# TensorE alone in text order in the phases of seven products, and another order of pieces in the convolution (a two-layer trunk on one core)

## The chip, the core and the metric

One core of a Trainium2 chip runs the whole program in one launch. Its engines are TensorE (PE in the profile; PEld is its weight load), VectorE (DVE), ScalarE (ACT), GpSimd (POOL) and SyncE (SP), which issues the transfers. Each engine works off its own list of instructions in order and waits on semaphores for the others. The metric is the device time of one execution in microseconds (us), as the median of several runs.

## What is computed

Two layers work on x of 1024 positions by 1024 channels in float32: the first mixes the positions by attention with a forgetting gate, the second by a convolution module, and after each mixer comes a gated MLP with a short convolution.

```
x = x + fox_attention(rms_norm(x))                 # layer 0, 16 heads of 64
x = x + conv_ffn(rms_norm(x))
x = x + conformer_conv(rms_norm(x))                # layer 1
x = x + conv_ffn(rms_norm(x))

def conformer_conv(h):                             # 1024 channels, 31 taps
    u = h @ w_pw1 + b_pw1
    a, g = split(u)
    u = causal_dwconv(a * sigmoid(g), w_dw) + b_dw
    return silu(rms_norm(u, ln_g)) @ w_pw2 + b_pw2

def conv_ffn(h):                                   # F = 2816, 3 taps
    u = causal_dwconv(h @ w_up, w_dw) + b_dw       # w_up: 1024 x 5632
    gate, val = split(u)
    return (silu(gate) * val) @ w_down             # w_down: 2816 x 1024
```

## The kernel before

**Products in three parts.** A float32 operand is split into a high part in TensorE's fp32r type (a cast on ScalarE, line 266) and a low part, the rest (a subtraction on GpSimd or VectorE, line 267). A product is then three matmuls (lines 272 to 274, `mm3`): high by high, low by high, high by low. Buffers of weights are few: 8 raw tiles of 256 KB (`raw`), 8 high and 8 low parts (`whi`, `wlo`).

**The up-projection in seven products.** `up` makes the product of a tile of 128 features by all 1024 positions with Strassen's scheme in Winograd's form: the 2x2 block product (halves of the 1024 inputs by halves of the positions) takes seven products of 12 matmuls each instead of eight. GpSimd makes the sums of the weights' quarters s1 to s4 (line 471). The sums on the activations' side are made once ahead, by `combine`. The 22 tiles (each: 128 gate features as upper row, 128 value features as lower row) go through this in a fixed order. TensorE's order in the steady state is product 6 of the next tile, 4 and 3 of the present one, then 5 and 7 of the next one; a "full" tile has products 1 and 2 besides. Products 6, 7 and 4 add up in one PSUM bank (`y`), 5 and 3 in another (`z`). Between them VectorE reads the bank's state: u2 after product 6 (line 533), u3 after product 7 (line 542), c22, the lower right block, from z and u3 (line 543). So product 4 can start only when u3 has been read out of `y`. After product 4 y gets its last addend (line 547), after product 3 z does (line 556).

Each of a tile's four blocks then goes through the three taps: ScalarE makes the last tap and the bias (line 483), copies or adds the two edge columns between the halves of positions (lines 486 and 491), VectorE adds the other two taps (line 493, twice). The gate's two blocks go through Silu on ScalarE (line 497), and VectorE multiplies gate by value (line 502); the result is stored in DRAM (`actd`, line 194).

**Early products.** Products 1 and 2 of a tile need no sums. `early` makes them ahead: beside `combine`, and in layer 1 also beside the convolution; ScalarE copies them out of PSUM (line 437), they are stored (`p1d`, `c11d`) and fetched again by the tile (line 476). Such a tile is called "ready" here; it has five products, and its x block comes from SBUF. In layer 0, 13 of 22 tiles are ready, in layer 1 all.

**Ahead.** In layer 0 each full tile also splits `AHEAD` = 4 weight tiles for later (`split_ahead`, lines 309 to 316): load, cast on ScalarE, subtraction on VectorE (line 315), store of the low part. They are the 32 tiles of the convolution's `w_pw1` (which both of its halves use) and the first 4 rows of the second down-projection. Who uses them later loads the low part instead of subtracting (line 85).

**The down-projection** (`down`) runs for each half of the positions and each half of the outputs over 22 rows: activations and weights are both split, VectorE making one low part and GpSimd the other; 12 matmuls a row.

**The convolution** (`conv`) runs for each half of the positions over 8 tiles of 128 channels. `glu` makes the two products (4 pieces, 48 matmuls) and then the gate piece: sigmoid on ScalarE (line 1045), the product u on VectorE (line 1048). `taps_of` does the 31 taps: 10 of them as products on ScalarE (line 1084) and sums on GpSimd (line 1085), 21 on VectorE (lines 1078 and 1080) in seven pieces, then the end piece: y, the sum of both (line 1092), its square on ScalarE (lines 1094 and 1097), added up on GpSimd (line 1098). In the list two pieces of taps stand to one of the next tile's `glu`; every 4 pieces of the first half's list one row of the second down-projection follows (`CONV_DOWN`), every 5 of the second half's list one early product (`CONV_FILL`).

**What sets the order.** The attention and its output projection are ordered by the compiler's scheduler. All that follows is a list of pieces (`pieces` and `trace`): loads stand ahead of splits, splits ahead of the work on TensorE, and the whole stretch stands in one `manual_schedule()`: every engine's list keeps the order of the text.

## Time and profile before

| | us |
|---|---|
| median of 3 runs | 2701.33 |
| range of the runs | 2698.57 to 2701.36 |
| the profiled execution | 2692.02 |
| its span | 2690.3 |
| PE busy in it | 2356.1 (88%) |
| DVE, ACT, POOL busy | 1616.4, 1381.5, 1401.8 |

The stretches, from the first and last instructions of their lines in the trace: attention and its output projection to 667 us; early products and `combine` to 742; tiles of layer 0's up-projection to 1211; first down-projection to 1339; first convolution with the second down-projection to 1641; second product of the convolution to 1663; second convolution to 1858; its norm, second product and `combine` to 2007; tiles of layer 1's up-projection to 2434; down-projections to the end. A busy PE in these lists is not PE at its peak: the end of a matmul is modelled, and at full clock matmuls start closer together than their listed lengths.

### The profile page before, as it was taken

Reading aid. Unit: us, or ns where it says so; the run is one execution under the profiler, and the core shown is the slowest. Engines: PE = TensorE matmul, PEld = TensorE weight load, DVE = VectorE, ACT = ScalarE, POOL = GpSimd, SP = SyncE. Lnnn points to the kernel's source line nnn. Section 1 sums busy time; section 2 is a strip of 40 time slices with the busy share of each in tenths; the row PEclk is TensorE's granted clock in tenths of the full one; section 3 lists DMA queues with packets and bytes.
Section 4 is the critical chain, followed back from the end, with each engine's and each line's share of the span. In section 5 each row is a group of like instructions: output and inputs, shape, how many; then the busy total and the mean of one; then the engine's idle time right before and its main releaser. Section 6 shows DMA issues by size and latency. Waiting matters only on the chain. (4 is left out here: it accounts for less than half of the span.)

```text
span 2690.3 us, 35380 instructions
## 1 busy us (share of the span) xinstructions
PE 2356.1 (88%) x11282; PEld 1993.4 (74%) x11282; DVE 1616.4 (60%) x2855; ACT 1381.5 (51%) x2956; POOL 1401.8 (52%) x1220
## 2 busy tenths in 40 slices
PE   7999999999987778889988978787977777778998
PEld 6899999977865667667866767676866666567887
DVE  5577777763745566665258973786475555555232
ACT  5566666653544445554455554555444444445443
POOL 2455554430165656655557764576255565554543
PEclk9999999999999989999999989898988888889999
DMA  4222222432633334556665446353543333335674
GB/s 118 58 77 82 82 80 69 166 113 85 221 110 99 110 98 146 160 171 228 200 212 163 147 133 196 110 164 113 189 129 102 107 105 98 98 117 193 194 256 157
DMA packets 355083, 366.70 MB, mean 136 GB/s; under 512 B 24872, under 2 KB 246864, under 8 KB 354896
## 3 DMA queue, kind: packets, MB, share of 16 engines
q1 hardware_dynamic: 354896, 364.44, 42.9%
q8 instruction: 89, 1.46, 0.2%
q14 instruction: 98, 0.80, 0.1%
HBM read 281.44 MB, written 74.51 MB: 132 GB/s over the span
## 5 line engine op out<-in xcount | busy, mean ns | idle before, releaser
L267 POOL TENSOR_TENSOR wlo<-raw,whi 128x512 fp32r<-128x512 f32 (+1 forms) x322 | 462.9, 1444 | 318.8 <-ACT whi L266 294.3
L266 ACT CAST whi<-raw 128x512 fp32r<-128x512 f32 (+2 forms) x544 | 326.2, 632 | 284.2 <-PE dn L273 193.8
L272 PE MATMUL y<-bhi,whi 128*128 128x512 f32 x528 | 239.0, 453 | 193.6 <-DVE u L542 179.2
L267 POOL TENSOR_TENSOR wlo<-s,whi 128x512 fp32r<-128x512 f32 x176 | 234.0, 1341 | 304.3 <-ACT whi L266 272.0
L267 DVE TENSOR_TENSOR wlo<-raw,whi 128x512 fp32r<-128x512 f32 (+1 forms) x222 | 187.3, 850 | 278.0 <-ACT whi L266 265.1
L272 PE MATMUL dn<-whi,whi 128*128 128x512 f32 x704 | 280.0, 398 | 16.7 <-ACT whi L266 10.6
L272 PEld LDWEIGHTS y<-bhi,whi 128*128 128x128 f32 x528 | 116.0, 220 | 235.7 <-ACT whi L266 181.8
L273 PE MATMUL dn<-wlo,whi 128*128 128x512 f32 x704 | 279.1, 396 | 12.0 <-POOL wlo L267 7.5
L274 PE MATMUL dn<-whi,wlo 128*128 128x512 f32 x704 | 278.4, 396 | 1.3 <-DVE wlo L267 1.3
L1080 DVE SCALAR_TENSOR_TENSOR cacc<-u,ctaps,cacc 128x512 f32<-128x512 f32 x320 | 241.7, 755 | 10.7
L273 PE MATMUL y<-blo,whi 128*128 128x512 f32 x528 | 232.2, 440 | 0.0
L274 PE MATMUL y<-bhi,wlo 128*128 128x512 f32 x528 | 230.3, 436 | 0.3 <-POOL wlo L267 0.3
L1085 POOL TENSOR_TENSOR pacc<-pacc,prod 128x512 f32<-128x512 f32 x144 | 193.0, 1340 | 51.1 <-ACT prod L1084 43.7
L266 ACT CAST whi<-s 128x512 fp32r<-128x512 f32 x176 | 104.5, 612 | 182.6 <-POOL s L471 182.6
L145 POOL TENSOR_SCALAR ss<-ss 128x4 f32<-128x4 f32 (+1 forms) x96 | 21.2, 221 | 327.2 <-ACT hn L160 178.6
L272 PE MATMUL pj<-whi,hthi 128*128 128x384 f32 (+1 forms) x512 | 180.0, 352 | 6.0 <-ACT sqr L736 3.5
L273 PE MATMUL pj<-wlo,hthi 128*128 128x384 f32 (+1 forms) x512 | 178.0, 348 | 0.5 <-DVE wlo L267 0.5
L274 PE MATMUL pj<-whi,htlo 128*128 128x384 f32 (+1 forms) x512 | 178.2, 348 | 0.0
L272 PEld LDWEIGHTS dn<-whi,whi 128*128 128x128 f32 x704 | 134.7, 191 | 48.4 <-ACT whi L266 12.6
L273 PEld LDWEIGHTS dn<-wlo,whi 128*128 128x128 f32 x704 | 134.9, 192 | 42.6 <-POOL wlo L267 9.7
L471 POOL TENSOR_TENSOR s<-raw,raw 128x512 f32<-128x512 f32 x88 | 116.8, 1327 | 83.6 <-DMA raw<-in_ffn_w_up_dram 60.3
L274 PEld LDWEIGHTS dn<-whi,wlo 128*128 128x128 f32 x704 | 135.0, 192 | 30.2 <-DVE wlo L267 1.8
(217 smaller groups left out, 6322.2 us busy)
## 6 DMA issues: line engine op xcount, KB each, us to landing
raw<-in_ffn_w_up_dram SPq DMA_DIRECT2D x246, 256.0 KB
raw<-actd SPq DMA_DIRECT2D x176, 256.0 KB
raw<-in_ffn_w_down_dram SPq DMA_DIRECT2D x176, 256.0 KB
raw<-in_conv_w_pw_dram SPq DMA_DIRECT2D x96, 256.0 KB
actd<-acc SPq DMA_DIRECT2D x88, 256.0 KB
wlo<-pwlo SPq DMA_DIRECT2D x64, 256.0 KB
raw<-in_fox_w_in_dram SPq DMA_DIRECT2D x64, 192.0 KB
xd<-x SPq DMA_DIRECT2D x24, 512.0 KB
```

Source lines behind the costliest of these rows:

```text
L145: nc.gpsimd.tensor_scalar(ss, ss, 1.0 / n, EPS, op0=ALU.mult, op1=ALU.add)
L266: self.nc.scalar.copy(hi, raw)
L267: (self.nc.vector if vector else self.nc.gpsimd).tensor_tensor(lo, raw, f32(hi), op=ALU.subtract)
L272: nc.tensor.matmul(out, lh, rh, start=start, stop=False, skip_group_check=more)
L273: nc.tensor.matmul(out, lh, rl, start=False, stop=False, skip_group_check=more)
L274: nc.tensor.matmul(out, ll, rh, start=False, stop=stop, skip_group_check=more)
L471: nc.gpsimd.tensor_tensor(st[o], *(st[m].rearrange("p a b -> p (a b)") if m[0] == "a" else st[m] for m in ((y, x) if o == "s4" else (x, y) ...
L1080: nc.vector.scalar_tensor_tensor(acc, win(j), tap(j), acc, op0=ALU.mult, op1=ALU.add)
L1085: nc.gpsimd.tensor_tensor(pacc, pacc, p, op=ALU.add)
```

## The change

1. `manual_schedule` is opened anew by a piece `order(...)`. In the two up-projections (from the end of `combine`) it names TensorE alone; ScalarE, VectorE, GpSimd and SyncE get the order that the compiler's scheduler gives them. After the first one all engines keep text order again; after the second one nothing is switched back, so the last two down-projections belong to it too. `combine` itself stays in text order, with two early products to each of its first six pieces and one to each of the last six (before: two to each).
2. In the convolution pieces of taps and of `glu` alternate one to one, so that the gate piece stands amid the taps; the square of a tile is a piece of its own, after the third piece of the next tile's taps. In the second half the products of two tiles come first.
3. `CONV_FILL` is (6, 1), `AHEAD` is 5, and the numbers of pieces around the second half are others.
4. The bias `b_pw2` is added by VectorE instead of GpSimd.

```diff
-CONV_FILL = (5, 1)
+CONV_FILL = (6, 1)
-AHEAD = 4
+AHEAD = 5
...
+    def order(self, *engines):
+        def run():
+            if self.region is not None:
+                self.region.__exit__(None, None, None)
+            self.region = self.tc.manual_schedule(engines=set(engines) if engines else None)
+            self.region.__enter__()
+        return Piece(run)
...
                 nc.vector.tensor_tensor(y, t["acc"], t["pacc"], op=ALU.add)
-                if ct == 0:
-                    nc.scalar.activation(st["sqa"], y, AF.Square)
-                else:
-                    sq = self.part("sq")
-                    nc.scalar.activation(sq, y, AF.Square)
-                    nc.gpsimd.tensor_tensor(st["sqa"], st["sqa"], sq, op=ALU.add)
             for i in range(0, nv, 3):
                 yield Piece(lambda i=i: some(i, min(i + 3, nv)))
+                if i == 6 and ct > 0:
+                    yield Piece(lambda: square(ct - 1))
             yield Piece(end)
...
         def first():
             yield from glu(0)
+            if h == 1:
+                yield from glu(1)
             for ct in range(KT):
-                if ct + 1 < KT:
-                    yield from alternate(taps_of(ct), glu(ct + 1), 2)
+                if ct + 1 < KT and (h, ct) != (1, 0):
+                    yield from alternate(taps_of(ct), glu(ct + 1), 1)
                 else:
                     yield from taps_of(ct)
+            yield Piece(lambda: square(KT - 1))
...
-        yield from both(T.combine(fac, keep), first, 1, 2)
+        combine = T.combine(fac, keep)
+        for n in (2, 1):
+            for _ in range(6):
+                yield from some(combine, 1)
+                yield from some(first, n)
         keep["stop"] = True
         yield from first
+        yield T.order(PE)
...
-                nc.gpsimd.tensor_tensor(xs[tb][:, m], xs[tb][:, m], b2[nh], op=ALU.add)
+                nc.vector.tensor_tensor(xs[tb][:, m], xs[tb][:, m], b2[nh], op=ALU.add)
...
     def pieces():
+        yield T.order()
         down0 = ffn_down(0, 0, xds[0], conv_norm)
         yield from ffn_up(0, keep, T.early(0, keep, w_up), down0, False)
+        yield T.order()
...
-        yield from turned(main1, 3)
+        yield from turned(main1, 2)
         yield from both(main1, first, *CONV_FILL)
+        yield from some(first, 6)
+        yield from some(norm1, 1)
         yield from some(first, 3)
-        yield from some(norm1, 1)
-        yield from some(first, 2)
...
-    ctx.enter_context(tc.manual_schedule())
```

**A ready tile.** VectorE's list amid layer 1's up-projection, from the taps of a tile's x block to u3 of the next tile. Names are the program's (u with three numbers fewer stands for u2 and u3; c is c22; p is the product p1; numbers after a name tell buffers apart). Before, as text:

```order
L493 SCALAR_TENSOR_TENSOR acc_21420<-x_21344,ffntab_158,acc_21420 128x511
L493 SCALAR_TENSOR_TENSOR acc_21420<-x_21344,ffntab_158,acc_21420 128x510
L493 SCALAR_TENSOR_TENSOR acc_21427<-y_21247,ffntab_158,acc_21427 128x511
L493 SCALAR_TENSOR_TENSOR acc_21427<-y_21247,ffntab_158,acc_21427 128x510
L502 TENSOR_TENSOR acc_21427<-acc_21420,acc_21427 128x512
L493 SCALAR_TENSOR_TENSOR acc_21434<-c_4363_21364,ffntab_158,acc_21434 128x511
L493 SCALAR_TENSOR_TENSOR acc_21434<-c_4363_21364,ffntab_158,acc_21434 128x510
L556 TENSOR_TENSOR z_21331<-z_21331,u_4345_21260 128x512
L493 SCALAR_TENSOR_TENSOR acc_21458<-z_21331,ffntab_158,acc_21458 128x511
L493 SCALAR_TENSOR_TENSOR acc_21458<-z_21331,ffntab_158,acc_21458 128x510
L502 TENSOR_TENSOR acc_21434<-acc_21458,acc_21434 128x512
L542 TENSOR_TENSOR u_4392_21504<-y_21388,p_4334_21226 128x512
```
After, as the scheduler has it (line 506 is the former 493, 515 the former 502, 560 the former 547, 569 the former 556, 555 the former 542):

```order
L506 SCALAR_TENSOR_TENSOR acc_21561<-x_21485,ffntab_158,acc_21561 128x511
L506 SCALAR_TENSOR_TENSOR acc_21561<-x_21485,ffntab_158,acc_21561 128x510
L560 TENSOR_TENSOR y_21388<-y_21388,p_4337_21226 128x512
L506 SCALAR_TENSOR_TENSOR acc_21568<-y_21388,ffntab_158,acc_21568 128x511
L569 TENSOR_TENSOR z_21472<-z_21472,u_4378_21401 128x512
L506 SCALAR_TENSOR_TENSOR acc_21568<-y_21388,ffntab_158,acc_21568 128x510
L506 SCALAR_TENSOR_TENSOR acc_21575<-c_4396_21505,ffntab_158,acc_21575 128x511
L515 TENSOR_TENSOR acc_21568<-acc_21561,acc_21568 128x512
L506 SCALAR_TENSOR_TENSOR acc_21575<-c_4396_21505,ffntab_158,acc_21575 128x510
L506 SCALAR_TENSOR_TENSOR acc_21599<-z_21472,ffntab_158,acc_21599 128x511
L506 SCALAR_TENSOR_TENSOR acc_21599<-z_21472,ffntab_158,acc_21599 128x510
L555 TENSOR_TENSOR u_4425_21645<-y_21529,p_4367_21367 128x512
```
The x taps stand ahead of y's last addend, z's addend has moved in between the two y taps, and u3 (the last row) stands directly behind z's taps: the gate product that stood ahead of it comes after it.

SyncE's list there, from one fetch of a product to the next. Before:

```order
L194 DMA actd_7968<-acc_21716 128x512
L476 DMA p_4454_21790<-p1d_16_8808 128x512
L291 DMA raw_21803<-in_ffn_w_up_dram 128x4x128
L291 DMA raw_21805<-in_ffn_w_up_dram 128x4x128
L291 DMA raw_21807<-in_ffn_w_up_dram 128x4x128
L291 DMA raw_21809<-in_ffn_w_up_dram 128x4x128
L194 DMA actd_7969<-acc_21850 128x512
L476 DMA x_21908<-c11d_15_8829 128x512
```
After (line 304 is the former 291, 489 the former 476, 195 the former 194):

```order
L304 DMA raw_21948<-in_ffn_w_up_dram 128x4x128
L195 DMA actd_7968<-acc_21850 128x512
L489 DMA p_4487_21931<-p1d_16_8808 128x512
L195 DMA actd_7968<-acc_21857 128x512
L304 DMA raw_21950<-in_ffn_w_up_dram 128x4x128
L304 DMA raw_22085<-in_ffn_w_up_dram 128x4x128
L304 DMA raw_22087<-in_ffn_w_up_dram 128x4x128
L489 DMA x_22049<-c11d_15_8829 128x512
L304 DMA raw_22089<-in_ffn_w_up_dram 128x4x128
```
The loads of weights no longer come four in a row: one of them stands behind both stores of gated activations, and the next fetch of an x block stands behind two more loads.

**A full tile.** VectorE's list in layer 0's up-projection, from u3 on. Before:

```order
L542 TENSOR_TENSOR u_2315_11892<-y_11753,p_2278_11717 128x512
L543 TENSOR_TENSOR c_2316_11893<-z_11863,u_2315_11892 128x512
L315 TENSOR_TENSOR araw_11739<-araw_11739,ahi_11919 128x512
L315 TENSOR_TENSOR araw_11745<-araw_11745,ahi_11931 128x512
L315 TENSOR_TENSOR araw_11751<-araw_11751,ahi_11937 128x512
L315 TENSOR_TENSOR araw_11810<-araw_11810,ahi_11943 128x512
L533 TENSOR_TENSOR u_2335_11962<-y_11949,p_2320_11913 128x512
L547 TENSOR_TENSOR y_11753<-y_11753,p_2278_11717 128x512
L493 SCALAR_TENSOR_TENSOR acc_11981<-y_11753,ffntab_145,acc_11981 128x511
```
After (328 is the former 315, 546 the former 533):

```order
L555 TENSOR_TENSOR u_2337_11972<-y_11830,p_2298_11788 128x512
L328 TENSOR_TENSOR araw_11814<-araw_11814,ahi_11999 128x512
L556 TENSOR_TENSOR c_2338_11973<-z_11943,u_2337_11972 128x512
L515 TENSOR_TENSOR acc_11869<-acc_11905,acc_11869 128x512
L328 TENSOR_TENSOR araw_11820<-araw_11820,ahi_12003 128x512
L328 TENSOR_TENSOR araw_11827<-araw_11827,ahi_12016 128x512
L328 TENSOR_TENSOR araw_11887<-araw_11887,ahi_12023 128x512
L328 TENSOR_TENSOR araw_11890<-araw_11890,ahi_12030 128x512
L546 TENSOR_TENSOR u_2358_12050<-y_12037,p_2342_11993 128x512
L560 TENSOR_TENSOR y_11830<-y_11830,p_2298_11788 128x512
L506 SCALAR_TENSOR_TENSOR acc_12069<-y_11830,ffntab_145,acc_12069 128x511
L506 SCALAR_TENSOR_TENSOR acc_12069<-y_11830,ffntab_145,acc_12069 128x510
```
Five ahead subtractions stand there instead of four, one of them ahead of c22; the gate product of the tile before has come in between. In the whole program layer 0 now has 10 ready and 12 full tiles (before 13 and 9): 6 early products fewer stand beside `combine`, and the second down-projection takes 28 of its 44 rows' low parts from DRAM (before 4).

**The first convolution.** VectorE's list from the end of one tile's taps to those of the next. Before:

```order
L1092 TENSOR_TENSOR y_14781<-cacc_14628,pacc_14629 128x512
L267 TENSOR_TENSOR wlo_14819<-raw_14680,whi_14818 128x512
L1048 SCALAR_TENSOR_TENSOR u_14830<-pw_2946_14643,cvec,sg_14828 128x512
L1078 TENSOR_SCALAR cacc_14834<-u_14830,ctaps 128x512
L1080 SCALAR_TENSOR_TENSOR cacc_14834<-u_14830,ctaps,cacc_14834 128x512 x5
L267 TENSOR_TENSOR wlo_14883<-raw_14746,whi_14882 128x512
L1080 SCALAR_TENSOR_TENSOR cacc_14834<-u_14830,ctaps,cacc_14834 128x512 x6
L267 TENSOR_TENSOR wlo_14938<-raw_14802,whi_14937 128x512
L1080 SCALAR_TENSOR_TENSOR cacc_14834<-u_14830,ctaps,cacc_14834 128x512 x9
```
After (1061 is the former 1048, 1091 the former 1078, 1093 the former 1080, 1105 the former 1092):

```order
L1061 SCALAR_TENSOR_TENSOR u_14756<-pw_2953_14662,cvec,sg_14754 128x512
L1091 TENSOR_SCALAR cacc_14760<-u_14756,ctaps 128x512
L1093 SCALAR_TENSOR_TENSOR cacc_14760<-u_14756,ctaps,cacc_14760 128x512 x14
L1061 SCALAR_TENSOR_TENSOR u_14929<-pw_2975_14769,cvec,sg_14927 128x512
L1093 SCALAR_TENSOR_TENSOR cacc_14760<-u_14756,ctaps,cacc_14760 128x512 x6
L1105 TENSOR_TENSOR y_14963<-cacc_14760,pacc_14761 128x512
L1091 TENSOR_SCALAR cacc_14967<-u_14929,ctaps 128x512
L1093 SCALAR_TENSOR_TENSOR cacc_14967<-u_14929,ctaps,cacc_14967 128x512 x11
```
The next tile's u is made amid the taps, so that the next tile's first tap follows y at once; and the subtractions of the down-projection's activations (line 267) are gone from this place, GpSimd makes them now.

10 lines of the change are left out of this document (added).

## The prediction

> **What bounds the kernel now.** I began with the page's costliest groups, where TensorE's idle time names its releaser, went on to the busy time by stretch, then to TensorE's waits and VectorE's timeline inside one tile of layer 1's up-projection.
>
> ```profile
> L272 PE MATMUL y<-bhi,whi 128*128 128x512 f32 x528 | 239.0, 453 | 193.6 <-DVE u L542 179.2
> ```
> ```profile
> core 0: us, PE busy (x) PEld busy (x) DVE busy (x) ACT busy (x) POOL busy (x), PEclk, DMA share, GB/s
> 975.00:1211.00 236.00, 203.74 (x816) 163.08 (x816) 154.23 (x192) 125.58 (x259) 137.62 (x104) 0.92 0.47 148
> 1404.00:1568.00 164.00, 139.34 (x561) 110.92 (x560) 145.62 (x188) 89.77 (x165) 122.33 (x91) 0.92 0.45 143
> 1706.00:1858.00 152.00, 125.07 (x528) 102.08 (x528) 125.30 (x178) 86.74 (x164) 114.72 (x90) 0.93 0.42 134
> 2007.00:2434.00 427.00, 328.94 (x1272) 262.22 (x1270) 245.18 (x318) 188.56 (x399) 241.70 (x181) 0.88 0.33 101
> ```
> ```profile
> PE y L272 <- DVE u L542: 95.7, 20, 5.1
> ```
>
> Of TensorE's idle time one wait stands out: product 4 waits for u3 (line 542), in the last row 20 times in layer 1, 95.7 us in all. The windows are full tiles of layer 0 (975), the two convolutions (1404, 1706) and layer 1's ready tiles (2007). In the last no engine is near its limit: DVE 57%, POOL 57%, PE 77% at a clock of 0.88. So a chain sets the time there. Its tile, on VectorE (start, length, and in brackets the idle time ahead and its releaser) and ACT:
>
> ```profile
> 2107.24 0.68 DVE L542 TENSOR_TENSOR u<-y,p 128x512 f32<-128x512 f32 x1
> 2107.96 0.70 DVE L543 TENSOR_TENSOR c<-z,u 128x512 f32<-128x512 f32 x1
> 2108.57 0.68 DVE L533 TENSOR_TENSOR u<-y,p 128x512 f32<-128x512 f32 x1
> 2113.03 0.70 DVE L547 TENSOR_TENSOR y<-y,p 128x512 f32<-128x512 f32 x1 [3.78 <-PE y L274]
> 2114.26 2.78 DVE L493 SCALAR_TENSOR_TENSOR acc<-x,ffntab,acc 128x511 f32<-128x511 f32 x2 [0.53 <-ACT acc L483]
> 2118.51 1.53 DVE L493 SCALAR_TENSOR_TENSOR acc<-y,ffntab,acc 128x511 f32<-128x511 f32 x2 [1.48 <-ACT edge L486]
> 2120.08 0.69 DVE L502 TENSOR_TENSOR acc<-acc,acc 128x512 f32<-128x512 f32 x1
> 2120.69 1.53 DVE L493 SCALAR_TENSOR_TENSOR acc<-c,ffntab,acc 128x511 f32<-128x511 f32 x2
> 2122.14 0.69 DVE L556 TENSOR_TENSOR z<-z,u 128x512 f32<-128x512 f32 x1
> 2124.86 1.53 DVE L493 SCALAR_TENSOR_TENSOR acc<-z,ffntab,acc 128x511 f32<-128x511 f32 x2 [2.04 <-ACT acc L491]
> 2127.16 0.69 DVE L502 TENSOR_TENSOR acc<-acc,acc 128x512 f32<-128x512 f32 x1 [0.76 <-ACT acc L497]
> 2127.76 0.68 DVE L542 TENSOR_TENSOR u<-y,p 128x512 f32<-128x512 f32 x1
> ```
> ```profile
> 2117.67 0.76 ACT L483 ACTIVATE acc<-y,ffntab 128x512 f32<-128x512 f32 x1
> 2118.33 0.15 ACT L486 COPY edge<-y 128x2 f32<-128x2 f32 x1
> ```
>
> From u3 to u3 it is 20.52 us: some 12 us of work and 8.6 us in five waits for PE or ACT, each at the head of a list that is worked off in order. From the x taps on the rows belong to the present tile; u3 in the last row is the next tile's, and its operands had long been there, as product 7's last matmul started at 2120.79 (below). So u3 is late only because of its place, and TensorE waits for it:
>
> ```profile
> 2108.07 0.77 PE L272 MATMUL y<-bhi,whi 128*128 128x512 f32 x1 [4.64 <-DVE u L542]
> 2109.06 0.63 PE L274 MATMUL y<-bhi,wlo 128*128 128x512 f32 x1
> 2118.30 0.39 PE L272 MATMUL y<-bhi,whi 128*128 128x512 f32 x1
> 2120.79 0.39 PE L274 MATMUL y<-bhi,wlo 128*128 128x512 f32 x1
> ```
>
> The last two rows are 11 starts apart: 0.226 us a matmul, 2.72 a product, **13.6 us for five products, 19.0 for seven**. After the wait of 4.64 us matmuls take 0.63 instead of 0.39 for a while. The wait and this slow start make up 20.5 less 13.6.
>
> **Ready tiles.** After the change VectorE's list is u3, the previous gate product, c22, u2, the x taps, y's addend, y tap, z's addend, y tap, c22 tap, gate product, c22 tap, z taps, u3. With the durations above: u3 0.68, c22 0.70, u2 0.68, addends 0.70 and 0.69, gate products 2 x 0.69, y, c22 and z taps 3 x 1.53, together 9.4; x taps 2.78 to 3.34, since one of them takes up to
>
> ```profile
> L493 DVE SCALAR_TENSOR_TENSOR acc<-x,ffntab,acc x42: 742/1083/1666, 2012.9 to 2421.9; 128x511 f32<-128x511 f32 x21, 128x510 f32<-128x510 f32 x21
> L315 DVE TENSOR_TENSOR araw<-araw,ahi x36: 677/1223/1840, 999.3 to 1193.6; 128x512 fp32r<-128x512 f32 x36
> ```
>
> One wait remains, from y's addend over ACT's 0.76 and 0.15 to y's first tap, about 1.0; PE's product 4 has ended by y's turn, and the other ACT results stand one or two operations ahead. That is 13.2 to 13.8, and with 0.04 for each of 14 handovers 13.8 to 14.3. The gate products read SBUF twice like the x taps and L315 (0.68 alone, up to 1.84 beside POOL), and POOL will be busy nearly always, so each can cost another 1.0: 13.8 to 16.3. TensorE's floor is 13.6, POOL's work 241.7/21 = 11.5. I take **15.0**, the middle: one of the two gate products falls into POOL's remaining pause, as ACT's casts, on which POOL waits, start only behind the x block.
>
> [...]
>
> With a PE wait near 1 us the slow start goes too; a pause of that size cost nothing in the convolution:
>
> ```profile
> 1453.42 0.50 PE L272 MATMUL pw<-hthi,whi 128*128 128x512 f32 x1 [0.96 <-ACT sg L1045]
> ```
>
> [...]
>
> **The sum.** The steps between tiles are counted by u3:
>
> ```profile
> L542 DVE TENSOR_TENSOR u<-y,p x13: 683/684/692, 750.3 to 996.9; 128x512 f32<-128x512 f32 x13
> L542 DVE TENSOR_TENSOR u<-y,p x10: 680/682/683, 996.9 to 1210.7; 128x512 f32<-128x512 f32 x10
> L542 DVE TENSOR_TENSOR u<-y,p x22: 683/684/693, 2006.9 to 2433.9; 128x512 f32<-128x512 f32 x22
> ```
>
> *Layer 1:* 21 steps in 427.0 us become 21 x 15.0 = 315: **-112**.
>
> *Layer 0:* 12 ready and 9 full steps take 246.6 + 213.8 = 460.4; a full one 23.8. Afterwards there are 9 and 12. A full tile's VectorE work is five L315 (at 1.22: 6.1) and x taps from PSUM (1.53, as the z taps) beside the 9.4, 17.0, plus handovers 0.8; in ACT's new list four casts
>
> ```profile
> L266 ACT CAST whi<-raw 128x512 fp32r<-128x512 f32 (+2 forms) x544 | 326.2, 632 | 284.2 <-PE dn L273 193.8
> ```
>
> of 0.63 stand between its work on c22 and on z, so that VectorE waits some 3 us there beside the 1.0: about 22. Ends: TensorE's 19.0, and 23.8 with one more L315, 25.0. I take 22.0: 9 x 15.0 + 12 x 22.0 = 399: **-61**.
>
> *Six early products fewer beside `combine`:* TensorE is full there;
>
> ```profile
> L437 ACT COPY ev<-e x24: 577/588/604, 677.0 to 736.7; 128x512 f32<-128x512 f32 x24
> ```
>
> 23 steps in 59.7 us are 2.6 each, 15.6 for six; `combine`'s VectorE chain hides perhaps a little: **-14** (0 to -16).
>
> *Convolutions:*
>
> ```profile
> L1092 DVE TENSOR_TENSOR y<-cacc,pacc x8: 683/692/692, 1404.1 to 1567.6; 128x512 f32<-128x512 f32 x8
> L1092 DVE TENSOR_TENSOR y<-cacc,pacc x8: 691/692/693, 1705.8 to 1857.9; 128x512 f32<-128x512 f32 x8
> 1453.40 0.75 DVE L1048 SCALAR_TENSOR_TENSOR u<-pw,cvec,sg 128x512 f32<-128x512 f32 x1 [1.79 <-ACT sg L1045]
> L1080 DVE SCALAR_TENSOR_TENSOR cacc<-u,ctaps,cacc 128x512 f32<-128x512 f32 x320 | 241.7, 755 | 10.7
> ```
>
> A tile takes 23.4 in the first and 21.7 in the second. VectorE's own part is 21 taps at 0.755 with 0.025 for each handover, y 0.69 and u 0.75: 17.9. Before, u stood behind y, and VectorE, ACT and TensorE, whose next products need the two banks that u reads, all stood still at each change of tile. With u amid the taps the banks come free half a tile earlier and VectorE goes from y to the next tap at once; the square costs the same, only later, where ACT need not wait for y. These waits go, and in the first half so do most subtractions of line 267 (3.5 a tile). There TensorE's 48 matmuls and 3.5 rows of 12, 90 x 0.226 = 20.3, become the bound: 7 x (23.4 - 20.6) = 20. In the second, with 48 and 2.3 x 12 matmuls (17.1), VectorE stays it: 7 x (21.7 - 18.6) = 22. I take **-22 for each** (-8 to -27); the first gains a little more by moving two rows forward.
>
> *The rest at nothing:* the adds of `b_pw2` (8 x 2) go from POOL to VectorE beside waits for the norm; if they aren't hidden, they cost 16 x 0.69 = 11, and if they free SyncE's stores sooner, they save the 4.49 us of the row quoted below. More early products ahead of the second norm are as many fewer beside `combine`: +-5. The second half's start, with two tiles' products first, I leave as it is: the norms and the first tile's taps fill it on VectorE in either order. The last down-projections keep nearly their order.
>
> Together -112 - 61 - 14 - 44 = -231: 2692.0 - 231 = 2461 for the profiled execution. The runs' median of 2701.3 lies 9.3 above it, so **2470**.
>
> **Rivals.** (1) *TensorE becomes the bound throughout.* For it: POOL has pauses and 13.6 lies only 1.4 below. Then 427 - 21 x 13.6 = 141, 460.4 - 9 x 13.6 - 12 x 19.0 = 110, 15, 25 and 26: -317, **2384**.
>
> (2) *The order is freed in name only.* u3 still stands behind z's taps, and only the wait for Silu and the gate product (0.76 + 0.69, 1.4 us) come off the chain. Then 21 + 9 steps give 42, the convolutions 30: **2629**. Against it: the order shows x taps and z's addend moved as well.
>
> [...]
>
> (4) *Slower: SyncE's list.* A weight load stands behind the stores of gated blocks and waits for a free raw buffer; the fetch of x stands behind it. The casts of these weights stand in ACT's list ahead of Silu, so a late load holds VectorE, and all four engines. Between freeing the buffer and needing its new content GpSimd has four operations:
>
> ```profile
> L471 POOL TENSOR_TENSOR s<-raw,raw 128x512 f32<-128x512 f32 x88 | 116.8, 1327 | 83.6 <-DMA raw<-in_ffn_w_up_dram 60.3
> ```
>
> 4 x 1.3 = 5.2. A landing, from issue to the matmul that waited for it, took at most 4.0:
>
> ```profile
> 1348.42 0.38 SPq L85 DMA_DIRECT2D wlo<-dnlo  x1
> ```
> ```profile
> 1352.40 0.80 PE L273 MATMUL dn<-wlo,whi 128*128 128x512 f32 x1 [4.49 <-DMA wlo<-dnlo]
> ```
>
> Every us above 5.2 is one more per tile; from 10.5 on a ready tile is no faster than now. At 12 a ready tile takes 21.8 and a full one, with nine loads on eight buffers, some 28: 21 x 21.8 - 427 = +31, 9 x 21.8 + 12 x 28 - 460 = +72, less 58 elsewhere: +45, **2746**. DMA shares of 0.33 to 0.47 speak against it.
>
> **Chances.** Forecast (2425 to 2515) 0.61, (1) 0.15, (3) 0.16, (2) 0.05, (4) 0.03. The range takes in most of (1) and (3): 2390 to 2575. A measurement of this kernel can tell about 0.2% from no change: faster 0.95, same 0.02, slower 0.03.
>
> **What would show it.** Right: u3 to u3 near 15 in layer 1, PE's wait for u below 1.5 us with 0.39 behind it, no wait for the gate between convolution tiles. [...] A full tile above 24 would sink layer 0's term.

## The result, and the profile after

The changed kernel takes **2409.55 us** (median of 4 runs, 2408.45 to 2414.33) against 2699.95 of the kernel before beside it (4 runs, 2692.03 to 2701.36): a ratio of 0.893, with a 95% interval of 0.891 to 0.896. The forecast was 2470 and the range 2390 to 2575. The profiled execution has a span of 2406.7 us against 2690.3, 283.6 less.

First the page of the profile after: the span, the busy times, and two of the costliest groups (line, engine, operation, names, shapes, count, busy time and mean, then idle time ahead and its releaser).

```profile
span 2406.7 us, 35521 instructions
...
PE 2272.0 (94%) x11282; PEld 1941.1 (81%) x11282; DVE 1635.2 (68%) x2861; ACT 1384.4 (58%) x2977; POOL 1401.7 (58%) x1214
...
L285 PE MATMUL y<-bhi,whi 128*128 128x512 f32 x528 | 211.1, 400 | 32.9 <-DVE u L555 18.5
...
L506 DVE SCALAR_TENSOR_TENSOR acc<-x,ffntab,acc 128x511 f32<-128x511 f32 x88 | 116.1, 1319 | 61.0 <-ACT edge L499 58.2
```

TensorE is now busy 94% of the span, and product 4's wait for u3 (line 555 now) has shrunk from 179.2 to 18.5 us. The x taps now stand 61.0 us idle, 58.2 of them for ScalarE (in the kernel before 32.7 in all). The same busy times by stretch: full tiles of layer 0, the two convolutions, layer 1's tiles.

```profile
core 0: us, PE busy (x) PEld busy (x) DVE busy (x) ACT busy (x) POOL busy (x), PEclk, DMA share, GB/s
...
861.00:1119.50 258.50, 240.51 (x1022) 195.15 (x1020) 183.98 (x248) 159.22 (x328) 167.50 (x126) 0.97 0.62 197
...
1307.00:1453.00 146.00, 135.25 (x575) 109.92 (x574) 131.02 (x173) 89.11 (x161) 120.50 (x93) 0.96 0.60 192
...
1592.00:1718.00 126.00, 115.76 (x511) 95.53 (x509) 119.00 (x161) 79.30 (x140) 111.58 (x88) 0.97 0.51 158
...
1868.00:2156.00 288.00, 287.48 (x1262) 236.16 (x1261) 260.76 (x317) 182.46 (x396) 252.76 (x180) 1.00 0.50 156
```

In layer 1's tiles TensorE is busy 287.48 of 288 us at a clock of 1.00; its list of waits has no row there. In the full tiles it is 18 us short. The steps are counted as before, by u3 and by y:

```profile
L555 DVE TENSOR_TENSOR u<-y,p x9: 679/681/692, 734.6 to 849.4; 128x512 f32<-128x512 f32 x9
...
L555 DVE TENSOR_TENSOR u<-y,p x13: 675/681/691, 861.4 to 1119.5; 128x512 f32<-128x512 f32 x13
...
L555 DVE TENSOR_TENSOR u<-y,p x22: 672/681/692, 1868.3 to 2156.5; 128x512 f32<-128x512 f32 x22
...
L1105 DVE TENSOR_TENSOR y<-cacc,pacc x8: 690/692/693, 1307.6 to 1452.7; 128x512 f32<-128x512 f32 x8
...
L1105 DVE TENSOR_TENSOR y<-cacc,pacc x8: 692/692/692, 1592.6 to 1718.3; 128x512 f32<-128x512 f32 x8
```

21 steps in 288.2 us make 13.72 for a ready tile of layer 1; the 12 full ones take 258.1, or 21.5 each. Beside the forecast:

| term | forecast, us | measured, us |
|---|---|---|
| layer 1, 21 ready steps | -112 | 288.2 - 427.0 = -138.8 |
| layer 0, 21 steps | -61 | 385.0 - 460.4 = -75.4 |
| six early products fewer ahead of the first u3 | -14 | 734.6 - 750.3 = -15.7 |
| first convolution | -22 | 145.1 - 163.5 = -18.4 |
| second convolution | -22 | 125.8 - 152.1 = -26.3 |
| the rest (here: 283.6 less the sum above) | 0 | -9.0 |

Now VectorE inside one ready tile of layer 1, from u3 to u3 (start, length, in brackets the wait ahead):

```profile
2005.69 0.68 DVE L555 TENSOR_TENSOR u<-y,p 128x512 f32<-128x512 f32 x1
2006.54 1.47 DVE L515 TENSOR_TENSOR acc<-acc,acc 128x512 f32<-128x512 f32 x1 [0.16 <-ACT acc L510]
2007.93 0.68 DVE L556 TENSOR_TENSOR c<-z,u 128x512 f32<-128x512 f32 x1
2008.53 0.68 DVE L546 TENSOR_TENSOR u<-y,p 128x512 f32<-128x512 f32 x1
2009.12 3.52 DVE L506 SCALAR_TENSOR_TENSOR acc<-x,ffntab,acc 128x511 f32<-128x511 f32 x2
2012.57 0.69 DVE L560 TENSOR_TENSOR y<-y,p 128x512 f32<-128x512 f32 x1
2014.16 0.75 DVE L506 SCALAR_TENSOR_TENSOR acc<-y,ffntab,acc 128x511 f32<-128x511 f32 x1 [0.90 <-ACT edge L499]
2014.82 0.69 DVE L569 TENSOR_TENSOR z<-z,u 128x512 f32<-128x512 f32 x1
2015.42 0.74 DVE L506 SCALAR_TENSOR_TENSOR acc<-y,ffntab,acc 128x510 f32<-128x510 f32 x1
2016.08 0.74 DVE L506 SCALAR_TENSOR_TENSOR acc<-c,ffntab,acc 128x511 f32<-128x511 f32 x1
2016.73 1.37 DVE L515 TENSOR_TENSOR acc<-acc,acc 128x512 f32<-128x512 f32 x1
2018.03 0.74 DVE L506 SCALAR_TENSOR_TENSOR acc<-c,ffntab,acc 128x510 f32<-128x510 f32 x1
2018.69 1.51 DVE L506 SCALAR_TENSOR_TENSOR acc<-z,ffntab,acc 128x511 f32<-128x511 f32 x2
2020.12 0.68 DVE L555 TENSOR_TENSOR u<-y,p 128x512 f32<-128x512 f32 x1
```

Of five waits two are left, 1.06 us together. This is one of the longer tiles, 14.43; steps of 14.4 and 13.1 alternate, as the first gate product takes 1.47 in the one and 0.69 in the other, and the x taps 3.52 and 3.00.

A full tile of layer 0 looks otherwise. Rows of GpSimd, ScalarE and VectorE from the timelines of one such tile:

```profile
982.43 1.85 POOL L484 TENSOR_TENSOR s<-raw,raw 128x512 f32<-128x512 f32 x1 [3.37 <-DMA raw<-in_ffn_w_up_dram]
```
```profile
985.68 0.62 ACT L279 CAST whi<-s 128x512 fp32r<-128x512 f32 x1 [4.30 <-POOL s L484]
...
988.95 0.78 ACT L496 ACTIVATE acc<-x,ffntab 128x512 f32<-128x512 f32 x1
```
```profile
989.88 0.75 DVE L506 SCALAR_TENSOR_TENSOR acc<-x,ffntab,acc 128x511 f32<-128x511 f32 x1 [6.08 <-ACT edge L499]
```

Read upwards: VectorE waits 6.08 us for ScalarE's part of the x block, which stands in ScalarE's list behind casts of weight sums, the first of which waits 4.30 for GpSimd's sum, which waits 3.37 for a late weight load.

### The profile page after: what moved, and what is told of

The parts are those of the page before. It is cut to its first block, busy times and chain, and to the rows that moved or that the text cites. A ratio compares the mean times of both kernels' runs of the same rounds, so it can differ in the third digit from the quotient of the medians.

```text
span 2406.7 us, 35521 instructions
## 1 busy us (share of the span) xinstructions
PE 2272.0 (94%) x11282; PEld 1941.1 (81%) x11282; DVE 1635.2 (68%) x2861; ACT 1384.4 (58%) x2977; POOL 1401.7 (58%) x1214
## 4 chain that ended last, share of the span: by engine, by line
PE 33%; DVE 15%; issue 2%; ACT 2%; DMA 1%; POOL 1%; SPq 0%; DVEq 0%; ACTq 0%; POOLq 0%
PE dn L286 7%; PE dn L287 7%; PE dn L285 7%; DVE cacc L1093 5%; DVE acc L506 4%; PE pw L287 1%; PE pw L286 1%; PE pw L285 1%; PE y L285 1%; PE y L286 1%; PE y L287 1%; DVE blo L413 1%; ACT acc L510 1%; DVE wlo L280 1%; PE z L286 1%
## 5 line engine op out<-in xcount | busy, mean ns | idle before, releaser
L279 ACT CAST whi<-raw 128x512 fp32r<-128x512 f32 (+2 forms) x520 | 314.2, 633 | 247.0 <-PE dn L286 185.1
L280 DVE TENSOR_TENSOR wlo<-raw,whi 128x512 fp32r<-128x512 f32 (+1 forms) x188 | 149.7, 803 | 244.1 <-ACT whi L279 234.2
L280 POOL TENSOR_TENSOR wlo<-s,whi 128x512 fp32r<-128x512 f32 x176 | 248.0, 1421 | 65.3 <-ACT whi L279 65.2
L285 PE MATMUL y<-bhi,whi 128*128 128x512 f32 x528 | 211.1, 400 | 32.9 <-DVE u L555 18.5
L1098 POOL TENSOR_TENSOR pacc<-pacc,prod 128x512 f32<-128x512 f32 x144 | 186.8, 1301 | 57.2 <-ACT prod L1097 49.7
L286 PE MATMUL y<-blo,whi 128*128 128x512 f32 x528 | 209.6, 397 | 9.1 <-DVE blo L413 9.1
L287 PE MATMUL y<-bhi,wlo 128*128 128x512 f32 x528 | 209.3, 396 | 0.0
L484 POOL TENSOR_TENSOR s<-raw,raw 128x512 f32<-128x512 f32 x88 | 124.9, 1419 | 87.5 <-DMA raw<-in_ffn_w_up_dram 50.0
L837 POOL TENSOR_SCALAR x<-x,nm 128x896 f32<-128x896 f32 (+7 forms) x128 | 100.8, 793 | 103.6 <-DVE nm L836 71.7
L506 DVE SCALAR_TENSOR_TENSOR acc<-x,ffntab,acc 128x511 f32<-128x511 f32 x88 | 116.1, 1319 | 61.0 <-ACT edge L499 58.2
```

What stands on the lines that cost most here:

```text
L279: self.nc.scalar.copy(hi, raw)
L280: (self.nc.vector if vector else self.nc.gpsimd).tensor_tensor(lo, raw, f32(hi), op=ALU.subtract)
L285: nc.tensor.matmul(out, lh, rh, start=start, stop=False, skip_group_check=more)
L286: nc.tensor.matmul(out, lh, rl, start=False, stop=False, skip_group_check=more)
L287: nc.tensor.matmul(out, ll, rh, start=False, stop=stop, skip_group_check=more)
L484: nc.gpsimd.tensor_tensor(st[o], *(st[m].rearrange("p a b -> p (a b)") if m[0] == "a" else st[m] for m in ((y, x) if o == "s4" else (x, y) ...
```

## The experiments

Each kernel was timed beside the kernel before on the same chip. All ratios are to that kernel, with their 95% interval; the changed kernel has 0.893 (0.891 to 0.896). Worked out from the profiles, by u3 and y as above (us; "full" is the mean step of a full tile; of layer 0's 21 steps 9 are full in `before` and `free_alone`, 12 in all others):

```
kernel          ready step   full   layer 0    first     second    span
                (layer 1)           tiles      conv.     conv.
before             20.33     23.8    460.3     163.6     152.1    2690.3
after              13.73     21.5    385.0     145.1     125.8    2406.7
text_all           20.34     25.3    490.7     145.1     125.8    2665.5
free_alone         13.73     19.0    335.6     163.6     152.1    2419.4
dve_free           18.64     24.2    459.9     145.1     125.5    2605.8
dve_text           17.06     22.7    431.1     145.1     125.7    2533.5
hand_u3            15.39     23.5    425.8     145.1     125.8    2506.4
dve_act_free       13.71     21.4    382.4     145.1     125.7    2407.8
ahead4             13.75     19.0    355.4     150.2     124.4    2382.3
raw9               13.72     19.0    353.6     145.2     125.5    2375.8
gate_behind        13.73     21.5    385.0     146.9     131.4    2410.3
square_behind      13.73     21.4    383.8     143.4     128.3    2424.5
vec_more           13.61     21.3    382.7     145.1     125.4    2403.9
raw9_free          13.72     19.0    354.7     147.9     133.5    2366.3
```

### The freed order, undone and alone

`text_all` undoes it, with all else of the change:

```diff
-        yield T.order(PE)
+        yield T.order()
         for p in T.up(l, fac, w_up, tabs[l], actd, keep):
```

> The changed kernel with all five engines in text order in the two up-projections too; everything else of the change stays. Theory A (the freed order makes the gain there): ready tiles fall back to 20.5 us and full ones to 25 (one more subtraction of 1.25), so 21 x 6.7 = 140 in layer 1 and 9 x 20.5 + 12 x 25 - 385 = 100 in layer 0 come back: about 2650, and TensorE waits for u3 some 100 us in layer 1. Rival B (the other edits make it: convolution, early products, AHEAD): below 2450.

Measured: 2666.58 us, ratio 0.988 (0.986 to 0.990), as theory A has it: ready tiles of 20.34 and full ones of 25.3, and in layer 1 TensorE waits 97.4 us for u3 again.

`free_alone` is the kernel before with `order(PE)` around its two up-projections (the last down-projections included) and no other edit of the change.

> The kernel before with the freed order of the two up-projections alone (and of the last down-projections behind them); convolution, CONV_FILL, AHEAD, early products and bias are the old ones. Theory A: layer 1 gives 139 and layer 0 with 12 ready steps of 13.8 and 9 full ones of 21 gives 105: about 2455. Rival B: above 2600. If the rest of the change pays only together with the freed order, this one and the run in text order don't add up: their two differences from the kernel before sum to clearly less than 290.

Measured: 2423.12 us, ratio 0.897 (0.895 to 0.900). So the freed order alone brings 278 of the 290 us, and all the other edits together 34 without it and 14 on top of it. The two gains alone add up to 312, more than 290, so the edits don't need each other. Theory A stands; its 2455 was too long, as the full tiles take 19.0 and not 21. That is the new thing: with the order alone TensorE has no wait in a full tile.

```profile
936.00:1088.00 152.00, 152.00 (x672) 125.85 (x671) 115.64 (x156) 101.91 (x209) 112.47 (x84) 1.00 0.62 198
```

These are eight full steps of 19.04 us, TensorE busy in 152.00 of 152.00. The changed kernel takes 21.5 for the same tile, so something else in the change costs 2.5 us there.

### Which engine's list

`dve_free` frees VectorE alone, `dve_text` the others without VectorE; `dve_act_free` frees VectorE and ScalarE:

```diff
-        yield T.order(PE)
+        yield T.order(PE, ET.Activation, ET.Pool, ET.SP)     # dve_free
+        yield T.order(PE, ET.DVE)                            # dve_text
+        yield T.order(PE, ET.Pool, ET.SP)                    # dve_act_free
```

> The changed kernel with TensorE, ScalarE, GpSimd and SyncE in text order in the up-projections and VectorE alone freed. Theory A, narrow form: VectorE's list is all that matters, within 2% of the changed kernel (2410 to 2460). Rival C (ACT's list matters too, since there Silu of x stands ahead of the last tap of y in text order and makes VectorE wait): ready tiles of 16 to 18, 2480 to 2580.

Measured: 2604.15 us, ratio 0.965 (0.962 to 0.967); slower than both theories said. The timelines of VectorE and ScalarE show what it waits for now:

```profile
2006.69 0.68 DVE L555 TENSOR_TENSOR u<-y,p 128x512 f32<-128x512 f32 x1
...
2008.55 1.53 DVE L506 SCALAR_TENSOR_TENSOR acc<-z,ffntab,acc 128x511 f32<-128x511 f32 x2
...
2018.47 2.82 DVE L506 SCALAR_TENSOR_TENSOR acc<-x,ffntab,acc 128x511 f32<-128x511 f32 x2 [2.32 <-ACT acc L496]
```
```profile
2016.58 0.62 ACT L279 CAST whi<-s 128x512 fp32r<-128x512 f32 x1 [4.75 <-POOL s L484]
2017.11 0.62 ACT L279 CAST whi<-raw 128x512 fp32r<-128x512 f32 x1
2017.63 0.81 ACT L496 ACTIVATE acc<-x,ffntab 128x512 f32<-128x512 f32 x1
```

The x taps need ScalarE's `acc` of x, and that stands, in text order, behind two casts of which the first waits 4.75 us for a sum of GpSimd. The fetch of that x block had been issued 11 us before (at 2006.54), and ScalarE's operation on it starts behind the casts with no wait of its own. The wait has moved from the head of one list to the head of another. And u3 stands ahead of the z taps here, earlier than in the changed kernel, yet a ready tile takes 18.64: an early place for u3 is not enough by itself.

> The opposite of dve_free: TensorE and VectorE in text order in the up-projections, ScalarE, GpSimd and SyncE freed. Theory D (VectorE's list is necessary, the others are needed to feed it): u3 stays behind the z taps and the gate product, and only some of VectorE's waits for ScalarE can go (0.5, 1.5, 0.8 a tile), so ready tiles of 17.7 to 20.5 us and 2570 to 2660. Theory E (the lists of ScalarE and GpSimd are the bigger part, since dve_free gave only 62 us): ready tiles below 16.5, below 2500.

Measured: 2535.19 us, ratio 0.940 (0.938 to 0.941), below theory D's range and above E's. Against `text_all` the lists of ScalarE, GpSimd and SyncE together thus give 131 us, VectorE's alone 62; neither is enough. (ScalarE's list was freed by itself in no run.) Here u3 still stands behind the z taps and the gate product, and what the ready tile lost (20.34 to 17.06) is for the most part waits of VectorE for ScalarE: 2.3 us a tile by the rows below, against 4.8 in the tile of before. VectorE's waits over 18 tiles (waited for, us in total, times, longest):

```profile
DVE y L560 <- PE y L287: 41.4, 17, 4.3
DVE acc L506 <- ACT acc L504: 27.8, 18, 1.6
DVE acc L515 <- ACT acc L510: 13.8, 18, 0.9
```

> VectorE and ScalarE freed in the up-projections, TensorE, GpSimd and SyncE in text order. In dve_free VectorE's x taps waited for ScalarE's last tap of x, and ScalarE for GpSimd's sums, at the head of its list. Theory D1 (those two lists are what matters): ready tiles of 13.8 to 14.5, 2410 to 2455. Rival D2 (GpSimd's or SyncE's order has to move too, since in text order the sums come late): ready tiles of 15.5 or more, 2470 or more.

Measured: 2409.27 us, ratio 0.893 (0.892 to 0.894), the changed kernel's own, and with ready tiles of 13.71 just under D1's bounds. Theory D1 holds: the lists of VectorE and ScalarE, freed together, are the whole gain of the freed order, 257 us against `text_all`; GpSimd and SyncE may stay in text order.

### u3's place, by hand

`hand_u3` keeps all engines in text order and moves the z block behind the next tile's u3. ScalarE's operations on that block and the store of its result move with it:

```diff
         shape = [P, 4, P]
+        held = []
...
                 nc.vector.tensor_tensor(w, st["z"], u3, op=ALU.add)
+                if held:
+                    held.pop()()
...
-                taps(0, 1, z)
-                gated(1)
+                def late():
+                    taps(0, 1, z)
+                    gated(1)
+                if f == NF - 1:
+                    late()
+                else:
+                    held.append(late)
```

> All engines in text order as in text_all, but in the text the taps and the gate product of a tile's z block stand behind u3 and c22 of the next tile. Nothing else moves. Theory A, narrow form (u3's place on VectorE alone sets the loop): ready tiles of 13.7 to 15.5 us, 2420 to 2470. Rival C (the scheduler's gain needs the other moves as well: x taps ahead of y, ACT's taps ahead of Silu, other places of the casts and loads): ready tiles of 17 or more, above 2530.

Measured: 2505.06 us, ratio 0.927 (0.925 to 0.930). Between the two ranges: the ready tile of 15.39 is what the narrow theory asks for, the whole isn't, as the full tiles stay at 23.5. Against `text_all` this one move is worth 2665.5 - 2506.4 = 159 us of span, 104 of them in layer 1. The rest of the way from 15.4 to 13.7 is three short waits for ScalarE in each tile, here over 14 tiles:

```profile
DVE acc L507 <- ACT edge L500: 21.6, 14, 1.5
DVE acc L516 <- ACT acc L511: 10.6, 14, 0.8
DVE acc L507 <- ACT acc L505: 9.0, 14, 0.6
```

41.2 us over 14 tiles are 2.9 a tile; in the tile of the changed kernel above 1.06 are left.

### What the fifth piece ahead costs

```diff
-AHEAD = 5
+AHEAD = 4                # ahead4
```

> The changed kernel with AHEAD = 4: eight loads into eight raw buffers in a full tile instead of nine. Theory F (the fifth piece ahead makes the full tile 21.6 instead of the 19.0 that free_alone showed): 12 full tiles of 19.0 to 19.3, -27 to -31 us, less at most 8 for 12 more subtractions in the second down-projection: 2378 to 2390. Rival G (free_alone has 19.0 for another reason, such as its early products): full tiles stay above 20.5, 2398 or more.

Measured: 2386.93 us, ratio 0.885 (0.884 to 0.886). Theory F holds: full tiles of 19.0, layer 0's tiles 29.6 us shorter; the first convolution 5.1 longer with 12 more subtractions in its rows.

```diff
-RAW_BUFS = 8
+RAW_BUFS = 9             # raw9, AHEAD = 5
...
-                    mine = st["e", s] = self.pp.tile([P, 2], F32, tag="edge", name=self.n("edge"), bufs=8)
+                    mine = st["e", s] = self.pp.tile([P, 2], F32, tag="edge", name=self.n("edge"), bufs=4)
```

> The changed kernel, AHEAD = 5 as it is, with nine raw buffers instead of eight (and four edge buffers instead of eight to make the room). Theory H (the fifth piece costs time because nine loads share eight buffers, so that a weight load is issued late and the casts, ScalarE's taps and VectorE's x taps wait behind it): full tiles of 19.0 to 19.8, 2378 to 2393. Rival I (the work itself: a fifth subtraction on VectorE, cast and store): full tiles of 21 to 22, 2402 to 2415.

Measured: 2377.73 us, ratio 0.883 (0.881 to 0.884). Theory H holds: with a ninth buffer the same five pieces a tile cost nothing. (`RAW_BUFS` also says how many loads may stand ahead of their splits in the text; the two effects were not parted.) GpSimd's wait for the weight load, over 10 full tiles of the changed kernel,

```profile
POOL s L484 <- DMA raw<-in_ffn_w_up_dram: 37.3, 10, 4.8
```

and over 10 of `raw9`, with its window (187.00 busy of 187.00, PE first):

```profile
POOL s L484 <- DMA raw<-in_ffn_w_up_dram: 5.5, 10, 1.0
```
```profile
883.00:1070.00 187.00, 187.00 (x826) 154.89 (x825) 146.97 (x198) 131.09 (x268) 148.67 (x111) 1.00 0.70 225
```

3.7 us a tile have become 0.6, and TensorE has no gap left. VectorE does the same subtractions in both, so their work was not the cause.

### The convolution, part by part

```diff
-                    yield from alternate(taps_of(ct), glu(ct + 1), 1)
+                    yield from alternate(taps_of(ct), glu(ct + 1), 2)      # gate_behind
```

> The changed kernel with two pieces of taps to one of glu again, so that the gate piece stands behind the end of a tile's taps; the later square and the two products ahead in the second half stay. Theory L (the gate's place is what both convolutions gained by): tiles back towards 23.4 in the first and 21.7 in the second half, +18 and +24: 2440 to 2455. Rival M (in the second half the products of two tiles ahead are what removes the wait): +10 to +20 in the first alone, 2420 to 2432.

Measured: 2411.35 us, ratio 0.893 (0.892 to 0.894), no different from the changed kernel. Both theories fall: the loops lengthen by 1.8 and 5.6 us, where 18 and 24 were expected.

```diff
                 nc.vector.tensor_tensor(y, t["acc"], t["pacc"], op=ALU.add)
+                square(ct)                                                 # square_behind
...
-                if i == 6 and ct > 0:
-                    yield Piece(lambda: square(ct - 1))
...
-            yield Piece(lambda: square(KT - 1))
```

> The changed kernel with the square directly behind y again. Theory N (as predicted, the square costs the same at either place, as its neighbours on ScalarE have time): within 5 us of the changed kernel, 2405 to 2415. Rival O (a square that waits for y holds up the products for GpSimd at the head of ScalarE's list): 1 us or more a tile, 2420 or more.

Measured: 2425.89 us, ratio 0.898 (0.897 to 0.899). 16 us slower, as rival O has it, but not by its mechanism: the loops take 143.4 and 128.3, against 145.1 and 125.8. In the profiled executions 5.8 us are lost ahead of the first u3, where the edit changes nothing; the rest between the loops, 146.6 against 139.9, and behind the second, 156.0 against 150.0. The busy times of the down-projection's `dn` alone, in the first loop and between the loops, show what moved there (PE and its count first). After the change:

```profile
1307.60:1452.70 145.10, 74.37 (x297) 57.63 (x295) 2.47 (x4) 0.96 0.61 192
1452.70:1592.60 139.90, 74.17 (x300) 58.48 (x300) 8.18 (x12) 0.89 0.50 158
```

In `square_behind`:

```profile
1311.60:1455.00 143.40, 70.03 (x273) 53.02 (x271) 2.47 (x4) 0.96 0.57 187
1455.00:1601.60 146.60, 79.15 (x324) 62.26 (x324) 7.92 (x12) 0.91 0.49 158
```

Two rows of 12 matmuls have moved out of the loop to the stretch behind it, and so have two early products (24 matmuls) out of the second loop. The square as a piece of its own makes each tile's list one piece longer, and a row follows every fourth piece, an early product every sixth. So the piece for the square pays by its count.

What the two edits may share is seen in the waits of the kernel before in its first convolution, of TensorE and of ScalarE:

```profile
PE pw L272 <- ACT sg L1045: 15.0, 5, 5.5
```
```profile
ACT sq L1097 <- DVE y L1092: 49.7, 6, 10.0
```

The square waits for y at the head of ScalarE's list, the next tile's sigmoid stands behind it, and the products behind the sigmoid. Either edit parts the two: the gate amid the taps puts the sigmoid ahead of the square, the later square takes the blocker away. In `gate_behind` TensorE has no wait for the sigmoid in the first loop, in `square_behind` 0.8 us. The changed kernel with both undone was not run; `free_alone`, which has both undone among others, shows the old loops, 163.6 and 152.1. So that this pair makes the gain is argued, not shown.

Other edits have a part in it. In the first loop VectorE makes 22 subtractions (`wlo`) in the kernel before, 7 in the changed one and 19 in `ahead4`, whose loop is 5.1 us longer; by that price the 15 that went are an estimated 6 of the 18.4 us. In the second loop 16 subtractions of a norm (`htlo`), 4.4 us of VectorE, have left the stretch from the first y to the last, and the products of two tiles stand ahead of it; what these are worth was not tried.

### Is VectorE the bound of a ready tile now?

```diff
                 nc.vector.tensor_tensor(y, y, st["p1"], op=ALU.add)
+                if l == 1:
+                    nc.vector.tensor_tensor(st["p1"], y, st["p1"], op=ALU.add)      # vec_more
```

> The changed kernel with one more VectorE instruction in each tile of layer 1, a sum of y and p1 behind y's last addend, 0.6 us from start to start; its result is not used. Theory J (VectorE's chain of 13.8 is by now the bound of a ready tile, TensorE's 13.6 close behind): steps of 14.3 to 14.5, +11 to +15 us: 2420 to 2425. Rival K (TensorE is the bound, and VectorE makes up for it in the 0.9 us that it waits for ScalarE): steps below 13.9, 2413 or less.

Measured: 2405.43 us, ratio 0.891 (0.890 to 0.893); not slower. A step takes 13.61, TensorE's 60 matmuls at 0.227, and no two matmuls of layer 1's tiles start more than 0.24 us apart. So TensorE is the bound here, as rival K says. In the changed kernel it nearly is: product 4 starts 0.2 to 0.3 us late in six of the 21 tiles (gaps too short for the list of waits), and these starts with the slower matmul behind each are 2.0 of the 2.4 us by which its tiles are longer. Theory J's times did not come, but its question stays open, for the scheduler had made another order and VectorE's work did not grow: the gate products became shorter. In layer 1, after the change and in `vec_more`:

```profile
L515 DVE TENSOR_TENSOR acc<-acc,acc 128x512 f32<-128x512 f32 x41 | 47.8, 1165 | 2.9 <-ACT acc L510 2.7
```
```profile
L515 DVE TENSOR_TENSOR acc<-acc,acc 128x512 f32<-128x512 f32 x41 | 30.9, 754 | 0.0
```

That is 0.82 us less for two gate products, against 0.6 more for the new sum. Why they became shorter is seen beside GpSimd's rows. After the change:

```profile
1933.98 1.38 DVE L515 TENSOR_TENSOR acc<-acc,acc 128x512 f32<-128x512 f32 x1
```
```profile
1933.52 1.29 POOL L484 TENSOR_TENSOR s<-raw,raw 128x512 f32<-128x512 f32 x1
```

In `vec_more`:

```profile
1946.71 0.68 DVE L515 TENSOR_TENSOR acc<-acc,acc 128x512 f32<-128x512 f32 x1
```
```profile
1945.52 1.30 POOL L280 TENSOR_TENSOR wlo<-s,whi 128x512 fp32r<-128x512 f32 x1
```

The first starts when GpSimd's instruction has 0.83 us to run, the second when it has 0.11. The lengths of the gate products follow one sum to 0.05 us, here in all 41 but one and in 66 of 68 of the changed kernel (861 to 2157 us): what is left of GpSimd's instruction at their start, plus 0.55, and never less than 0.68. The three others start within 0.03 us of GpSimd's instruction; they take 0.68, and in the two of the changed kernel GpSimd's instruction takes 1.85 and 1.86 in place of 1.29. So the new order set the gate products near the end of GpSimd's instructions.

### A faster version

`raw9_free` is `raw9` without the piece that brings text order back after the first up-projection:

```diff
         yield from ffn_up(0, keep, T.early(0, keep, w_up), down0, False)
-        yield T.order()
         yield Piece(fetch_b2)
```

> raw9 with TensorE alone in text order in the first down-projections and the convolution too. Theory P (what is left there are chains: the norms, VectorE's 21 taps a tile, TensorE's matmuls): within 15 us of raw9's 2378 either way. Rival Q (there too waits stand at the head of a list: TensorE is 24 and 21 us short of full between the convolutions and after the second): 2335 to 2360.

Measured: **2366.19 us**, ratio 0.877 (0.876 to 0.878), the fastest of all. Theory P's bound of 15 us holds, 11.5 less than `raw9`; that all is chains does not follow, as rival Q's stretches did give way. The convolutions get longer, by 2.7 and 8.0 us, the stretches behind them shorter, 139.5 to 130.5 and 149.5 to 138.1. Which of the moves in those stretches does it was not tried.

## Why the prediction was right, and where it was off

**What bounds the kernel: right.** Waits at the heads of lists were the matter, and not work: with the order freed alone 278 us go. But "u3 is late only because of its place" is too narrow. The z block moved behind u3 by hand does take the ready tile from 20.34 to 15.39. With VectorE alone freed, though, u3 stands earlier still and the tile takes 18.64, and with the lists of the other three freed it falls to 17.06 without any move of u3. In the changed kernel u3 has passed one gate product only; what went are VectorE's waits, 8.6 us a tile before and 1.06 after, as ScalarE's list now has its results ready in time. The prediction's sum rested on just that, on the new list with one wait left.

**Ready tile, 15.0: too long by 1.3, the largest error (27 us in layer 1).** VectorE's list and the size of the lengthening beside GpSimd were right: one wait of 0.9 for ScalarE, gate products with a mean of 1.165 in layer 1, so 2 x 0.48 = 0.96 over their 0.69 where 1.0 was allowed. What failed is "0.04 for each of 14 handovers". The lengths of the rows of the tile above add up to 14.26, with its waits 15.32, but from u3 to u3 it is 14.43: listed lengths overlap. 15.32 - 14.43 = 0.89 us less over the 13 rows, where 0.56 more were added; 15.0 - 1.45 gives 13.55. The rows of before that the prediction quotes have it: c22 and u2 start 0.61 apart, at a length of 0.70. The figure that counts is from start to start. With that VectorE's chain comes down to TensorE's 13.6, which the prediction had as a floor 1.4 below; in layer 1 TensorE is all but the bound.

**Full tile, 22.0: right in size (21.5) by luck, wrong in cause.** It was reckoned as VectorE's own work with 3 us of casts in ScalarE's list. The runs with 4 pieces or 9 buffers show that neither that work nor the casts bind: the tile then takes 19.0, TensorE's floor. The 6 us wait at the x taps comes from a load that is late because nine loads share eight buffers. That mechanism stands in the prediction, as rival 4, where it was to make the kernel slower; it was real, but in the full tiles alone and with 3.7 us a tile of waiting for the load.

**Combine, -14: right** (-15.7; runs with the same six products fewer have their first u3 up to 6 us later), but not a gain: the three tiles that became full take the time back.

**Convolutions, -22 each: right in sum (-44.7) and in the steps of a tile (20.7 and 18.0, forecast 20.6 and 18.6), the cause half wrong.** "Before, u stood behind y" put the wait down to the gate's place alone. Moving the gate back costs 3.6 us of span in all. By the waits of before the blocker was the square at the head of ScalarE's list, which either edit parts from the sigmoid (argued, as said above); and the prediction's "the square costs the same, only later" missed that the square's piece also lets two more rows of the down-projection fit into the first loop.

**The rest at nothing: right enough.** Of the 9.0 us, 5 were gained between the last u3 of layer 0 and the first y, 6 behind the last u3, where the freed order reaches the down-projections too, and 3 were lost around the convolutions.

**Rivals.** (1) TensorE as the bound throughout came nearly true in layer 1 of the changed kernel, and in the full tiles only with 4 pieces or 9 buffers; that its 2384 is near `ahead4` (2387) and `raw9` (2378) is partly chance, as these are other kernels. (2) is right that u3 still stands behind z's taps, but the waits ahead of it are gone too, and the steps are 13.7. (3), to which the upper end of the range goes back, had gate products and x taps lengthened beside GpSimd by more than came: gate products took 0.68 to 1.47 in layer 1, a pair of x taps up to 3.52. The extra of a gate product was what was left of GpSimd's instruction at its start, less 0.13 us: 0.48 in the mean in layer 1 and 0.8 at most, where a GpSimd instruction takes 1.29, and the steps stayed at 13.7. No run shows a gate product that waits out a whole one each time, nor what in the chip makes it longer. (4) is in the full tile above.

## What to carry to other kernels

When no engine is near its limit and one wait stands out, look for an operation whose operands have long been there: its place in the list may be the cost, and a move in the text can be worth much (u3's place alone 159 us of span here). Free (or reorder) the lists that feed each other together: freeing one of two leaves much of the wait at the head of the other (62 or 131 us here, 257 together). Count loads against buffers in the longest tile before adding work ahead to it (nine loads on eight buffers: 21.5 us a full tile here, on nine 19.0), and add up VectorE's time from start to start, not by listed lengths (14.43 against 15.32 us in the tile above).

## What the runs showed that was not expected

- Freed lists can change as a whole with one edit: 21 more VectorE instructions in layer 1 made its tiles 0.11 us shorter each (13.72 to 13.61), as the gate products came to start near the end of GpSimd's instructions. A difference of a few us between two versions under a scheduler need not come from the edit's own cost.
- A wait at the head of a list costs by what stands behind it: with VectorE alone freed, ScalarE's cast waited 4.75 us for a sum, and x's tap, which had no wait of its own, stood behind it and started 1.05 us after that cast.
- What a wait cost TensorE beyond itself was not the same below and above 2 us. In ten full tiles of the changed kernel (904 to 1104 us) it waited 0.7 to 2.6 us for u3. Behind the five waits of up to 1.9 us matmuls were back at 0.22 to 0.24 from start to start from the second one on. Of the five from 2.0 to 2.6 us, four were followed by seven or eight matmuls at about 0.43, at once or up to six matmuls later, as the 4.64 us of before were, and one of 2.38 was not. So slow matmuls came also behind a wait of 2.04, less than half the 4.64 that the prediction quotes. The granted clock was 0.97 there and 0.88 in the ready tiles of before.
